# A two-block network on one core: gated linear attention over pairs of chunks, normalised tiles in full value from ACT, and a table that shifts the planner's order

## The chip, the core and the metric

The kernel runs on one core of a Trainium2 chip. The engines are named as in the profile: PE multiplies matrices (PEld loads its weights), DVE works on vectors, ACT evaluates functions and casts, POOL (GpSimd) does some of the element-wise work, and SP issues DMAs. The metric is the device time of one run in microseconds (us); lower is better.

## What is computed

512 tokens of width 1024 go through two networks in a row, with float32 inputs and outputs. The first has two layers: a short convolution with a SwiGLU feed-forward stage (`ffn0` below), then a forgetting attention of 16 heads ("fox" in the code) with a second one (`ffn1`). Each sub-block ends with a layer norm over the residual. The second network has a mixing block of four heads of latent attention (MLA) beside four heads of gated linear attention, a third feed-forward stage (`ffn2`) and a gated projection. The part that the change rewrites is the gated linear attention, which runs once forward and once backward over the tokens:

```python
def gla_chunkwise(q, k, v, logf):            # CHUNK = 64, 8 chunks
    b = jnp.cumsum(logf.reshape(B, H, N, CHUNK, DK), axis=3)
    b_last = b[:, :, :, -1:, :]
    b_mid = b[:, :, :, CHUNK // 2 - 1:CHUNK // 2, :]
    A = einsum('bhntd,bhnsd->bhnts', q * exp(b - b_mid), k * exp(b_mid - b)) * mask
    o_intra = einsum('bhnts,bhnsv->bhntv', A, v)
    kv = einsum('bhnsd,bhnsv->bhndv', k * exp(b_last - b), v)
    # scan over chunks: state = exp(b_last) * state + kv; s_before is the state ahead of a chunk
    o_inter = einsum('bhntd,bhndv->bhntv', q * exp(b), s_before)
    return (o_intra + o_inter).reshape(B, H, S, DV)
```

## The kernel before

Activations lie transposed, 128 features on the partitions and 512 tokens along the free axis. A float32 product of full size is made of three fp32r matmuls, (high, high), (low, high) and (high, low): every weight unit `raw` of 128x1024 is cast by ACT to `whi`, and `wlo` = `raw` - `whi` is made by DVE or POOL; an activation tile is split in the same way into `...h` and `...l`. The smaller products of the gated linear attention are plain float32 matmuls.

The program is not written in the order in which it runs. Class `Build` records some ten thousand operations in a `Recorder`; `plan()` is a list scheduler that goes through a model of the engines with a cost for each operation and picks, on each engine, the ready operation with the lowest `prio`; `issue()` emits them in that order. Hence nearly every instruction has one line in the profile, that of `issue()` (L575), and a load of ACT's function table has L578. The priority is

```python
        op.prio = op.i - op.shift - OFFSETS.get(op.group, 0)
```

where `op.i` is the place in the recorded program, and `OFFSETS` is empty, so the order is that of the recording as far as data, buffers and engines allow. The planner may give some of DVE's `tensor_tensor` operations to POOL (`to_pool`); it lets no POOL operation start while a DVE operation with two SBUF inputs runs, and the other way round. `issue()` puts a table load right behind the last ACT operation that uses the old table. PSUM has 8 banks in classes `g`, `s` and `o`; four weight units (`WB`) are held at once.

What the change touches, by names in the profile:

- `split_scaled` is the end of each layer norm. For a tile `x` (features 128, tokens 256) ACT writes `hm0h`, `hm1h`, ... (the normalised tile times gain plus offset, rounded to fp32r); DVE writes the same in full value as `hm00e`, `hm10e`, ..., and subtracts, giving `hm0l`, `hm1l`, .... `ln_tiles` calls it 16 times in the norms behind the convolution block, `ffn0` and the attention; the queries' input `hq` takes it 8 times at 512 tokens.
- `gla_prep` makes, for head h and direction d, the decayed tiles from the running sum `b`: `gl01qi`, `gl01bm` (queries and keys relative to the middle of a chunk), `gl01bl` (keys to the end of a chunk), `gl01qb` (queries from the start of a chunk).
- `gla_scores` multiplies queries and keys over 128 tokens at a time, four matmuls into `gs01A`; `copy_predicated` with the mask `gmask` keeps the two 64x64 blocks on the diagonal, in their triangle. `gs01kt` transposes `gl01bl`, and ACT copies it to `gs01kd`.
- `gla_states` multiplies keys and values of each 64-token chunk (`gl01kv`, seven matmuls over 64 partitions, in two PSUM banks), makes seven states `gl01st` (one ACT copy and six DVE `scalar_tensor_tensor`, each needing the one before), and adds to the output `gpo` four matmuls of the masked scores `gat` with the values and seven of 64 columns with the states.
- In the mixing block `gt` are the gate projections, `gvt` the transposed values, `MS` the scores of MLA with `kns`, `krs` (keys) and `qns`, `qrs` (queries), `mx` the row maxima of MLA's softmax, `rqn`, `rkn` and `gr` sums for norms, `mx0` to `mx6` also (with h and l) the split outputs of the heads, and `wo` the output projection `w_o2`, of which partial sums start before all heads are done. `ffn2` starts with `pg` and `pu`.
- In the attention of block 1, `pk`, `pq`, `pv` are projections, `S` the scores, `Pa`, `Pm`, `Pb` the softmax parts after DVE has multiplied them by the reciprocal sums, `tp` their transposes, `PT` the split transposes, `po` the products with the values, and `Ftp` the transpose of the running sum `F` of the forget gates.

Of the kernel before, what the change touches and what calls it, by code (L numbers as in the profile page):

```python
# [85 lines left out]
    ("SP", "ACT"): 130, ("SP", "DVE"): 130, ("SP", "PE"): 130, ("SP", "POOL"): 130, ("SP", "SP"): 130,  # L86
}
FREE_LAT = {"g": 220, "s": 220, "o": 220, "whi": 200, "wlo": 200}
OFFSETS = {}
LOOK = 4000  # L90
DMA_LOOK = 250
POOL_LAG = -1000.0
# [101 lines left out]
class Recorder:  # L194
# [96 lines left out]
    def cost(self, op, ins, outs):  # L291
        n = op.name
        size = 1
        for d in outs[0].shape[1:] if outs and isinstance(outs[0], View) else ():
            size *= d
        if n == "dma_start":
            v = next(x for x in outs + ins if isinstance(x, View))
            byts = 4
            for d in v.shape:
                byts *= d  # L300
            op.dma = byts / 359.0
            return {"SP": 60, "ACT": 60, "POOL": 1040}[op.eng]
        if op.eng == "PE":
            dt = ins[0].dtype
            if n == "transpose":
                return 109
            if dt == F32:
                return 4 + max(4 * size / 2.4, 156)
            return 13.4 + max(size / 2.4, 95) if dt == F32R else 3 + size / 2.4
        psum = any(x.tile.cls in PSUM_CLS for x in ins)  # L310
        cols = sum(1 for x in ins if isinstance(x, View) and x.idx.size == 1)
        if op.eng == "ACT":
            return (51 if psum else 94) + 0.8333 * size + 93 * (cols + ("accum_out" in op.kw))
        if op.eng == "POOL":
            return 200 + 2.13 * size if n == "tensor_tensor" else 36 + 0.8333 * size
        if n in ("tensor_tensor_reduce", "tensor_reduce"):
            size = int(ins[0].idx.size)
        if n == "tensor_tensor_reduce":
            return 180 + 1.0417 * size + 61 * cols
        if n in ("tensor_scalar", "tensor_copy", "memset") and not psum:  # L320
            return 68 + 0.5208 * size + 61 * cols
        if n == "reciprocal":
            return 68 + 6.4 * size
        return 68 + 1.0417 * size + (61 * cols if size > 1 else 0)
# [264 lines left out]
class Build:  # L589
# [291 lines left out]
    def split_scaled(self, d, g, b, hl, sl, name):  # L881

        nc = self.nc
        nc.scalar.activation(hl[0][:, sl], d[:, sl], AF.Identity, bias=b, scale=g)
        e = self.f(name + "e", (P, sl.stop - sl.start))
        nc.vector.tensor_scalar(e, d[:, sl], g, b, ALU.mult, ALU.add)
        nc.vector.tensor_tensor(hl[1][:, sl], e, hl[0].bitcast(F32)[:, sl], ALU.subtract)

    def scaled(self, d, g, b, sl=slice(0, T)):
# [841 lines left out]
    def mla_scores(self, h, proj):  # L1731
# [2 lines left out]
        scale = float(192 ** -0.5)  # L1734
        mx = self.small(f"mx{h}", 4)
        rs = self.small(f"mrs{h}", 4)
        Ps = []
        for i in range(4):
            tb = slice(i * P, (i + 1) * P)
# [77 lines left out]

    def gla_prep(self, h, gates):

        nc = self.nc  # L1820
        kl, q, _, _ = gates
        out = []
        for d in range(2):
            k, b = kl[d]
            nm = f"gl{h}{d}"
            step = 1 - 2 * d
            mid, last = (31, 63) if d == 0 else (32, 0)
            b3 = b.chunks(64)
# [12 lines left out]
            self.act(bl, bl, AF.Exp)  # L1841
            nc.vector.tensor_tensor(bl, bl, k, ALU.mult)
            self.act(b, b, AF.Exp)
            qb = self.f(nm + "qb")
            nc.vector.tensor_tensor(qb, b, q, ALU.mult)
            out.append((qi, bm, bl, b, qb))
        return out

    def gla_scores(self, h, prep):
# [1 line left out]
        nc = self.nc  # L1851
        res = []
        for d in range(2):
            qi, ki, kd_, _, _ = prep[d]
            nm = f"gs{h}{d}"
            pa = self.ps("s", nm + "A", (P, 4, P))
            for p in range(4):
                sl = slice(p * P, (p + 1) * P)
                nc.tensor.matmul(pa[:, p, :], ki[:, sl], qi[:, sl], start=True, stop=True)
            nc.vector.copy_predicated(self.at[d], self.gmask[:, d:d + 1, :].to_broadcast((P, 4, P)), pa)  # L1860
            kd = self.f(nm + "kd", (P, 4, P))
            nc.scalar.copy(kd, self.to_token_ps(kd_, nm + "kt"))
            res.append(kd)
# [5 lines left out]
    def gla_states(self, h, gates, prep, kds):  # L1869
# [1 line left out]
        nc = self.nc  # L1871
        v = gates[2]
        po = self.ps("o", f"gpo{h}")
        first = True
        for d in range(2):
            b, qb = prep[d][3:]
            nm = f"gl{h}{d}"
            kd = kds[d]
            last = 63 * (1 - d)
            order = list(range(8)) if d == 0 else list(range(7, -1, -1))  # L1880

            pk = [self.ps("s", nm + f"kv{i}", (P, 4, P)) for i in range(2)]
            for c in order[:7]:
                rw = slice(64 * (c % 2), 64 * (c % 2) + 64)
                nc.tensor.matmul(pk[c % 2][:, c // 2, :], kd[rw, c // 2, :], v[rw, c // 2, :],
                                 start=True, stop=True)
            for p in range(4 if d == 0 else 0):
                nc.tensor.matmul(po[:, p * P:(p + 1) * P], v[:, p, :], kds[2][:, p, :],
                                 start=first, stop=False)
                first = False  # L1890
            st = [self.f(nm + f"st{i}", (P, 4, P)) for i in range(2)]
            S = None
            for i, c in enumerate(order[:7]):
                new = st[i // 4][:, i % 4, :]
                kvc = pk[c % 2][:, c // 2, :]
                if S is None:
                    nc.scalar.copy(new, kvc)
                else:
                    col = c * 64 + last
                    nc.vector.scalar_tensor_tensor(new, S, b[:, col:col + 1], kvc, ALU.mult, ALU.add)  # L1900
                S = new
                n = order[i + 1]
                nc.tensor.matmul(po[:, n * 64:(n + 1) * 64], S, qb[:, n * 64:(n + 1) * 64],
                                 start=False, stop=(d == 1 and i == 6))
        return po

    def gla_out(self, h, gates, po):
# [144 lines left out]
```

## Time and profile before

| | |
|---|---|
| Median of the runs | 1939.76 us (1939.32 to 1940.83, 3 runs) |
| Profiled execution: device time | 1939.52 us |
| Profiled execution: span, first to last instruction | 1937.8 us |
| Outside the span | 1.7 us |
| PE busy | 1893.9 us (98%) |
| DVE busy | 1284.3 us (66%) |
| ACT busy | 817.4 us (42%) |
| POOL busy | 190.3 us (10%) |
| Mean granted clock of PE | 0.989 |

A busy PE is not a PE at its peak: records of consecutive matmuls overlap, and at half clock each lasts longer. So the starts of consecutive matmuls give what one costs. The stages follow each other in time: convolution block to about 203 us, `ffn0` to 550, attention of block 1 to 835, `ffn1` to 1215, mixing block to 1529, `ffn2` and the gated projection to the end.

### The profile page before, as it was taken

What the parts mean: (1) busy time and instruction counts of PE and PEld (TensorE: products, weight loads), DVE (VectorE), ACT (ScalarE), POOL (GpSimd) and SP (SyncE); (2) the same over time, 40 slices, a digit from 0 to 9 for tenths busy, and PEclk for the clock granted to TensorE, in tenths of its full rate; (3) what the DMA queues carried; (4) which work ended last, traced back from release to release, by engine and by line L of the source; (5) the groups of instructions that cost most, each with busy time, mean ns of one, the idle gap of its engine ahead of it and who ended that gap; (6) DMA issues with size and microseconds to landing.
All of it is one profiled execution on the core that took longest, in us unless ns stands there. A gap on an engine that the chain in (4) does not pass through costs nothing.

```text
span 1937.8 us, 24555 instructions
## 1 busy us (share of the span) xinstructions
PE 1893.9 (98%) x9382; PEld 1593.3 (82%) x9382; DVE 1284.3 (66%) x2208; ACT 817.4 (42%) x1344; POOL 190.3 (10%) x148
## 2 busy tenths in 40 slices
PE   9999999999999989999999999999999999999999
PEld 7888888888888778898888888877877888888887
DVE  8877976566579788894533335999898644334445
ACT  5322523122346667553322232686684533123333
POOL 0000100000010332210000000132151000000000
PEclk9999999999999899999999999999998999999999
DMA  9675277566434112323222222422111222222232
GB/s 350 224 249 173 99 241 251 187 233 228 142 108 153 58 64 88 120 66 131 99 94 96 97 98 79 140 82 82 44 55 44 98 98 98 98 98 94 94 139 76
DMA packets 76470, 245.55 MB, mean 127 GB/s; under 512 B 8496, under 2 KB 9776, under 8 KB 76352
## 3 DMA queue, kind: packets, MB, share of 16 engines
q1 hardware_dynamic: 76352, 243.98, 36.6%
q8 instruction: 73, 1.20, 0.3%
q14 instruction: 45, 0.37, 0.1%
HBM read 235.53 MB, written 8.42 MB: 126 GB/s over the span
## 4 chain that ended last, share of the span: by engine, by line
PE 57%; DVE 7%; ACT 2%; issue 1%; DVEq 0%; ACTq 0%
PE pu L575 12%; PE pg L575 12%; PE pd L575 9%; PE gt L575 4%; PE ffn_down L575 2%; PE wo L575 2%; PE pl L575 2%; PE attn_o L575 1%; DVE axr L575 1%; PE pv L575 1%; PE po L575 1%; PE pq L575 1%; PE MS L575 1%; PE tp L575 1%; PE pk L575 1%; PE S L575 1%
## 5 line engine op out<-in xcount | busy, mean ns | idle before, releaser
L575 ACT CAST whi<-raw 128x1024 fp32r<-128x1024 f32 (+1 forms) x313 | 326.1, 1043 | 598.5 <-PE pd L575 139.1
L575 DVE TENSOR_TENSOR wlo<-raw,whi 128x1024 fp32r<-128x1024 f32 (+1 forms) x286 | 349.8, 1224 | 321.0 <-ACT whi L575 316.9
L575 POOL TENSOR_TENSOR wlo<-raw,whi 128x1024 fp32r<-128x1024 f32 x27 | 65.4, 2423 | 1281.7 <-ACT whi L575 1251.5
L575 DVE CUSTOM_DVE_ANT_0 aj<-ada,cact,adab 128x1024 bf16<-128x1024 f32 x96 | 126.3, 1322 | 30.0 <-DMA ada<-in_wada 29.4
L575 DVE TENSOR_TENSOR s<-pu,s 128x512 f32<-128x512 f32 x44 | 30.1, 689 | 76.5 <-PE pu L575 76.5
L575 DVE TENSOR_TENSOR S<-S,sq 128x512 f32<-128x512 f32 (+1 forms) x62 | 36.7, 591 | 1.6 <-ACT sq L575 1.4
L575 ACT ACTIVATE s<-s 128x512 f32<-128x512 f32 x22 | 13.9, 632 | 54.1 <-DVE s L575 54.1
L575 ACT ACTIVATE s<-pg 128x512 f32<-128x512 f32 x44 | 26.0, 591 | 23.2 <-PE pg L575 23.0
L575 DVE CUSTOM_DVE_ANT_0 G<-S,G 128x128 f32<-128x128 f32 (+3 forms) x64 | 30.6, 484 | 1.6 <-PE S L575 0.9
L575 DVE TENSOR_TENSOR xr<-pd,xr 128x512 f32<-128x512 f32 x16 | 11.0, 690 | 26.9 <-PE pd L575 26.9
L575 DVE TENSOR_SCALAR G<-Fm,fneg 128x128 f32<-128x128 f32 x64 | 25.9, 410 | 0.9 <-PE po L575 0.5
L575 ACT ACTIVATE sq<-axr 128x256 f32<-128x256 f32 (+1 forms) x33 | 15.1, 466 | 23.1 <-DVE axr L575 23.1
L575 DVE TENSOR_SCALAR G<-Fb,fneg 128x128 f32<-128x128 f32 (+2 forms) x48 | 23.6, 491 | 1.3 <-ACT Pa L575 0.6
L575 DVE TENSOR_TENSOR s<-pg,rfr 128x512 f32<-128x512 f32 x22 | 15.2, 691 | 12.0 <-PE pg L575 12.0
L575 DVE TENSOR_TENSOR u<-pu,rfr 128x512 f32<-128x512 f32 x22 | 15.2, 691 | 11.8 <-PE pu L575 11.7
L575 POOL TENSOR_TENSOR Fm<-Fb,cmask 128x512 f32<-128x512 f32 x14 | 18.6, 1334 | 27.7 <-DVE PT_2l L575 9.1
L575 PE MATMUL tp<-ident,Pa 128*128 128x128 f32 x64 | 17.2, 294 | 3.2 <-DVE Pa L575 3.1
L575 PE MATMUL pg<-hm0l,whi 128*128 128x512 f32 (+1 forms) x48 | 18.0, 376 | 1.9 <-DVE hm0l L575 1.9
L575 PE MATMUL pg<-hm0h,whi 128*128 128x512 f32 (+1 forms) x48 | 18.0, 378 | 1.3 <-ACT hm0h L575 1.3
L575 ACT ACTIVATE Pa<-G,negm 128x128 f32<-128x128 f32 (+1 forms) x32 | 16.2, 505 | 6.8 <-DVE negm L575 4.7
L575 ACT ACTIVATE sq<-x 128x256 f32<-128x256 f32 (+1 forms) x19 | 9.8, 518 | 21.6 <-DVE x L575 21.5
L575 PE MATMUL pg<-hm0h,wlo 128*128 128x512 f32 (+1 forms) x48 | 18.0, 376 | 0.6 <-DVE wlo L575 0.6
(3680 smaller groups left out, 6298.7 us busy)
## 6 DMA issues: line engine op xcount, KB each, us to landing
raw<-in_wpack SPq DMA_DIRECT2D x309, 512.0 KB, 3.5
ada<-in_wada SPq DMA_DIRECT2D x96, 512.0 KB, 4.2
ada<-in_wada SPq DMA_DIRECT2D x32, 256.0 KB, 6.0
Fb<-fd SPq DMA_DIRECT2D x16, 256.0 KB, 4.5
x<-in_xT SPq DMA_DIRECT2D x8, 256.0 KB, 6.0
pd<-pple SPq DMA_DIRECT2D x8, 256.0 KB, 6.0
xd<-x SPq DMA_DIRECT2D x8, 256.0 KB, 2.6
axr<-xd SPq DMA_DIRECT2D x8, 256.0 KB, 5.1
```

The lines of the kernel that those rows point to most:

```text
L575: getattr(getattr(nc, op.unit), op.name)(*[get(x) for x in op.args], **{k: get(x) for k, x in op.kw.items()})
```

## The change

Four parts. First, `OFFSETS` gets some 150 entries, one per group of operations, from -1420 to 5570 places; a positive one lets the group go earlier. This moves instructions on every engine. Second, two of the planner's costs are raised: that of small float32 matmuls and that of the scan. Third, `split_scaled` writes the full value with a second ACT activation in place of DVE's `tensor_scalar`. Fourth, the gated linear attention takes chunks in pairs of 128 tokens: the prepared keys and queries reach to the ends of a pair (six products of 256 elements and one of 4 columns, `dec`, in place of two of 512), each direction adds four matmuls `gs01A<-gl01x` (64 columns by 64) for the block of scores between the two chunks of a pair, two memsets per head widen the mask, `gl01kv` are three matmuls over all 128 partitions in one bank, and there are three states and three matmuls of 128 columns with them. The four `gat` matmuls stand first.

```diff
-OFFSETS = {}
+OFFSETS = {
+    "attn_o_0": 830, "attn_o_1": -20, "attn_o_2": 300, "attn_o_3": 30, "attn_o_ln0": -20, "attn_o_ln1": -20,
...
+    "q2": -80, "q3": 50, "q5": -10, "q6": 3750, "q7": 950, "sc1": -20, "sc2": 20, "sc3": -80, "sc4": -50,
+    "sc5": 70, "sc6": 2420, "score0": 650, "score1": -130, "score2": 50, "score3": 300, "state0": 4020,
...
-                return 4 + max(4 * size / 2.4, 156)
+                return 4 + max(4 * size / 2.4, 193)
...
+        if n == "tensor_tensor_scan":
+            return 68 + 2.0833 * size
...
-        nc.vector.tensor_scalar(e, d[:, sl], g, b, ALU.mult, ALU.add)
+        nc.scalar.activation(e, d[:, sl], AF.Identity, bias=b, scale=g)
...
+        nc.gpsimd.memset(self.gmask[:64, 0, 64:], 1)
+        nc.gpsimd.memset(self.gmask[64:, 1, :64], 1)
...
-            nc.vector.tensor_tensor(bl, bl, k, ALU.mult)
             self.act(b, b, AF.Exp)
+            bp, lp = b.chunks(P), bl.chunks(P)
+            x = self.f(nm + "x", (P, 2, 256))
+            kx, qx = x[:, 0, :].chunks(64), x[:, 1, :].chunks(64)
+            nc.vector.tensor_tensor(kx, lp[:, :, near], k3[:, :, near], ALU.mult)
+            nc.vector.tensor_tensor(lp[:, :, far], lp[:, :, far], k3[:, :, far], ALU.mult)
+            nc.vector.tensor_tensor(lp[:, :, near], kx, bp[:, :, e1:e1 + 1].to_broadcast((P, 4, 64)), ALU.mult)
+            nc.vector.tensor_tensor(qx, bp[:, :, far], q3[:, :, far], ALU.mult)
             qb = self.f(nm + "qb")
-            nc.vector.tensor_tensor(qb, b, q, ALU.mult)
-            out.append((qi, bm, bl, b, qb))
+            qp = qb.chunks(P)
+            nc.vector.tensor_tensor(qp[:, :, near], bp[:, :, near], q3[:, :, near], ALU.mult)
+            nc.vector.tensor_tensor(qp[:, :, far], qx, bp[:, :, e0:e0 + 1].to_broadcast((P, 4, 64)), ALU.mult)
+            dec = self.small(nm + "dec", 4)
+            nc.vector.tensor_tensor(dec, bp[:, :, e0], bp[:, :, e1], ALU.mult)
+            out.append((qi, bm, bl, dec, qb, x))
...
+            for p in range(4):
+                sl = slice(p * 64, (p + 1) * 64)
+                nc.tensor.matmul(pa[near, p, far], x[:, 0, sl], x[:, 1, sl], start=True, stop=True)
...
-            pk = [self.ps("s", nm + f"kv{i}", (P, 4, P)) for i in range(2)]
-            for c in order[:7]:
-                rw = slice(64 * (c % 2), 64 * (c % 2) + 64)
-                nc.tensor.matmul(pk[c % 2][:, c // 2, :], kd[rw, c // 2, :], v[rw, c // 2, :],
-                                 start=True, stop=True)
...
+            pk = self.ps("s", nm + "kv", (P, 4, P))
+            for c in order[:3]:
+                nc.tensor.matmul(pk[:, c, :], kds[d][:, c, :], v[:, c, :], start=True, stop=True)
+            st = self.f(nm + "st", (P, 4, P))
...
-            for i, c in enumerate(order[:7]):
+            for i, c in enumerate(order[:3]):
...
-                    nc.vector.scalar_tensor_tensor(new, S, b[:, col:col + 1], kvc, ALU.mult, ALU.add)
+                    nc.vector.scalar_tensor_tensor(new, S, dec[:, c:c + 1], pk[:, c, :], ALU.mult, ALU.add)
...
-                nc.tensor.matmul(po[:, n * 64:(n + 1) * 64], S, qb[:, n * 64:(n + 1) * 64],
-                                 start=False, stop=(d == 1 and i == 6))
+                nc.tensor.matmul(po[:, n * P:(n + 1) * P], S, qb[:, n * P:(n + 1) * P],
+                                 start=False, stop=(d == 1 and i == 2))
```

What the table does to the order is seen at three places. The first is PE near the end of the mixing block, ahead of the scores `MS` of MLA's last head. Before, one matmul of the output projection stands there:

```order
L575 MATMUL gs30A_13103<-gl30qi_12803,gl30bm_12582 128x128 x4
L575 MATMUL gs30kt_13119<-ident_74,gl30bl_12588 128x128 x4
L575 MATMUL gs31A_13125<-gl31qi_13047,gl31bm_13044 128x128 x4
L575 MATMUL gs31kt_13133<-ident_74,gl31bl_13051 128x128 x4
L575 MATMUL wo2_13140<-mx0h_12823,whi227_12425 128x512
L575 MATMUL gl30kv0_13148<-gv3_12596,gs30kd_13127 128x128 x4
L575 MATMUL MS3_0_13157<-kns3h_13142,qns3h_13091 128x512
L575 MATMUL MS3_0_13157<-kns3l_13154,qns3h_13091 128x512
```

Now:

```order
L606 MATMUL wo2_13086<-mx4h_12713,wlo228_12591 128x512
L606 MATMUL wo0_13056<-mx2h_12879,whi228_12569 128x512
L606 MATMUL wo1_13066<-mx2h_12879,whi228_12569 128x512
L606 MATMUL wo2_13086<-mx2h_12879,whi228_12569 128x512
L606 MATMUL wo4_13160<-mx0h_12432,whi231_13121 128x512
L606 MATMUL wo4_13160<-mx0l_12824,whi231_13121 128x512
L606 MATMUL MS3_0_13168<-kns3h_13165,qns3h_13151 128x512
L606 MATMUL MS3_0_13168<-kns3l_13170,qns3h_13151 128x512
L606 MATMUL MS3_0_13168<-kns3h_13165,qns3l_13162 128x512
```

Ahead of `MS3_0` there now stands a run of matmuls of the output projection `wo`, of which only the last are shown (32 from the second `rkn3ps` on; before there is one), and the scores `gs30A` and `gs31A` of the linear attention are apart from it.

The second is ACT at the layer norm behind the convolution block; `out1r` and `out1a` belong to its second half of tokens. Before:

```order
L575 ACTIVATE hm0h<-x_123,m0B,m0G 128x256
L575 ACTIVATE hm1h<-x_195,m0B,m0G 128x256
L575 ACTIVATE conv_out1r_1889<-conv_outvar_1859 128x256
L575 ACTIVATE conv_out1r_1889<-conv_out1r_1889 128x256
L578 ACT_TABLE_LOAD
L575 ACTIVATE conv_out1a<-conv_out1r_1889 128x256
L575 ACTIVATE hm2h<-x_235,m0B,m0G 128x256
```

Now:

```order
L606 ACTIVATE hm0h<-x_123,m0B,m0G 128x256
L606 ACTIVATE hm00e<-x_123,m0B,m0G 128x256
L606 ACTIVATE conv_out1r_1884<-conv_outvar_1863 128x256
L606 ACTIVATE hm1h<-x_194,m0B,m0G 128x256
L606 ACTIVATE conv_out1r_1884<-conv_out1r_1884 128x256
L609 ACT_TABLE_LOAD
L606 ACTIVATE hm10e<-x_194,m0B,m0G 128x256
L606 ACTIVATE conv_out1a<-conv_out1r_1884 128x256
L606 ACTIVATE hm2h<-x_234,m0B,m0G 128x256
```

Each rounded tile (`hm0h`) is followed by its full value (`hm00e`), and the table load that stood behind both `hm0h` and `hm1h` now stands between `hm1h` and `hm10e`.

The third is PE in the attention of block 1, where the first transpose `tp` of the first pair of heads stands. Before:

```order
L575 MATMUL pv_0_5453<-whi_5320,hk5h 128x256
L575 MATMUL pv_0_5453<-wlo_5338,hk5h 128x256
L575 MATMUL tp_0_5567<-ident,Pa_5402 128x128
L575 MATMUL pv_0_5453<-whi_5320,hk5l 128x256
L575 MATMUL pv_1_5466<-whi_5320,hk5h 128x256
L575 MATMUL pv_1_5466<-wlo_5338,hk5h 128x256
```

Now:

```order
L606 MATMUL pk_5327<-hk4h,wlo_5149 128x512
L606 MATMUL S_1_5551<-k1a,q1a 128x256
L606 MATMUL S_1_5551<-k1l,q1az 128x256
L606 MATMUL pk_5327<-hk5h,whi_5132 128x512
L606 MATMUL pk_5327<-hk5l,whi_5132 128x512
L606 MATMUL tp_0_5562<-ident,Pa_5393 128x128
L606 MATMUL pk_5327<-hk5h,wlo_5149 128x512
L606 MATMUL tp_0_5562<-ident,Pm_5439 128x128
```

Before, the transpose stands among the value projections `pv`; now all of these are ahead of it, the scores `S` of the next heads are too, and the key projection `pk` stands beside it.

## Rows read from the trace of the kernel before

**Rows 1.** The page, part 1: busy time, share of the span and instructions of each engine.
```profile
PE 1893.9 (98%) x9382; PEld 1593.3 (82%) x9382; DVE 1284.3 (66%) x2208; ACT 817.4 (42%) x1344; POOL 190.3 (10%) x148
```

**Rows 2.** Windows of the span: window, length; busy us per engine, granted clock, DMA.
```profile
610.00:700.00 90.00, 81.42 (x412) 67.10 (x412) 71.65 (x190) 51.50 (x121) 31.53 (x21) 0.89 0.31 103
...
1405.00:1450.00 45.00, 41.67 (x300) 34.36 (x297) 40.71 (x84) 38.54 (x77) 25.44 (x19) 1.00 0.17 59
1450.00:1475.00 25.00, 20.77 (x83) 17.67 (x83) 22.86 (x36) 9.50 (x19) 9.07 (x7) 0.66 0.13 43
...
1530.00:1900.00 370.00, 370.00 (x1634) 306.39 (x1633) 168.61 (x194) 117.60 (x140) 4.79 (x2) 1.00 0.29 103
```

**Rows 3.** The same view, of four stretches in which TensorE's clock was halved.
```profile
647.90:658.10 10.20, 9.59 (x32) 7.00 (x31) 8.38 (x33) 3.72 (x12) 0.00 (x0) 0.50 0.01 5
688.80:695.70 6.90, 5.28 (x18) 4.11 (x19) 5.81 (x19) 1.80 (x4) 1.42 (x4) 0.51 0.00 0
1450.00:1460.20 10.20, 10.12 (x46) 9.89 (x46) 10.07 (x21) 6.10 (x12) 4.85 (x5) 0.50 0.01 2
1467.10:1473.90 6.80, 5.91 (x14) 4.65 (x15) 5.35 (x10) 1.56 (x4) 0.00 (x0) 0.50 0.45 154
```

**Rows 4.** Waits of PE: who waited for whom: us in total, times, longest us.
```profile
PE tp L575 <- DVE Pm L575: 3.5, 2, 2.9
PE tp L575 <- DVE Pa L575: 3.1, 4, 1.5
...
PE Ftp L575 <- DVE F L575: 2.5, 1, 2.5
PE MS L575 <- DVE kns3l L575: 2.4, 1, 2.4
...
PE gpo L575 <- DVE gl20st L575: 1.9, 1, 1.9
PE MS L575 <- DVE mx L575: 1.8, 1, 1.8
```

**Rows 5.** Timeline of 1455 to 1475 us: start, us, engine, operation, names, [idle before].
```profile
1456.36 0.68 DVE L575 TENSOR_TENSOR gl31bm<-gl31bm,gz 128x512 f32<-128x512 f32 x1
...
1459.35 1.73 POOL L575 TENSOR_TENSOR mx0l<-mo,mx0h 128x512 fp32r<-128x512 f32 x1
...
1460.30 0.60 PE L575 MATMUL gs31kt<-ident,gl31bl 128*128 128x128 f32 x4
...
1463.23 1.75 DVE L575 TENSOR_TENSOR kns3l<-kn,kns3h 128x512 fp32r<-128x512 f32 x1
...
1465.03 0.50 PE L575 MATMUL MS<-kns3l,qns3h 128*128 128x512 f32 x1 [2.37 <-DVE kns3l L575]
```

**Rows 6.** Timeline of PE, second head of the gated linear attention.
```profile
1425.85 1.16 PE L575 MATMUL gl11kv<-gv,gs11kd 64*128 64x128 f32 x14
...
1429.44 1.16 PE L575 MATMUL gpo<-gat,gv 128*128 128x128 f32 x8 [0.84 <-DVE gat L575]
...
1433.33 1.73 PE L575 MATMUL gpo<-gl11qb,gl11st 128*128 128x64 f32 x14
```

**Rows 7.** The states of one direction, by tile: duration in ns, minimum, median, maximum.
```profile
L575 DVE SCALAR_TENSOR_TENSOR gl20st<-gl20st,sg_0e,gl20kv x6: 330/333/333, 1449.3 to 1451.9; 128x128 f32<-128x128 f32 x6
```

**Rows 8.** Timeline of 202 to 210 us, the layer norm behind the convolution block.
```profile
203.11 0.60 ACT L575 ACTIVATE hm0h<-x,m0B,m0G 128x256 fp32r<-128x256 f32 x1
...
203.86 0.69 DVE L575 TENSOR_SCALAR hm00e<-x,m0G,m0B 128x256 f32<-128x256 f32 x1
...
205.07 1.28 ACT L578 ACT_TABLE_LOAD   x1
...
205.41 0.41 DVE L575 TENSOR_TENSOR hm1l<-hm10e,hm1h 128x256 fp32r<-128x256 f32 x1
...
206.72 0.28 PE L575 MATMUL pg<-hm1l,whi 128*128 128x256 f32 x1
```

**Rows 9.** Timeline of PE in the attention of block 1: the first transpose.
```profile
638.62 0.30 PE L575 MATMUL tp<-ident,Pa 128*128 128x128 f32 x1 [0.76 <-DVE Pa L575]
```

More of the change, by code (lines that the diff above doesn't have):

```diff
@@ L88 @@
 FREE_LAT = {"g": 220, "s": 220, "o": 220, "whi": 200, "wlo": 200}
-OFFSETS = {}
+OFFSETS = {
[27 rows of a table added]
+}
 LOOK = 4000
@@ L1821, in gla_prep @@
         kl, q, _, _ = gates
+        q3 = q.chunks(P)
         out = []
@@ L1827, in gla_prep @@
             mid, last = (31, 63) if d == 0 else (32, 0)
-            b3 = b.chunks(64)
+            near, far = slice(64 * d, 64 * d + 64), slice(64 - 64 * d, P - 64 * d)
+            e0, e1 = (63, 127) if d == 0 else (64, 0)
+            b3, k3 = b.chunks(64), k.chunks(P)
             nc.vector.tensor_tensor_scan(b[:, ::step], self.cmk, b[:, ::step], 0.0, ALU.mult, ALU.add)
@@ L1853, in gla_scores @@
         for d in range(2):
-            qi, ki, kd_, _, _ = prep[d]
+            qi, ki, kd_, _, _, x = prep[d]
             nm = f"gs{h}{d}"
+            near, far = slice(64 * d, 64 * d + 64), slice(64 - 64 * d, P - 64 * d)
             pa = self.ps("s", nm + "A", (P, 4, P))
@@ L1873, in gla_states @@
         po = self.ps("o", f"gpo{h}")
-        first = True
+        for p in range(4):
+            nc.tensor.matmul(po[:, p * P:(p + 1) * P], v[:, p, :], kds[2][:, p, :],
+                             start=(p == 0), stop=False)
         for d in range(2):
-            b, qb = prep[d][3:]
+            dec, qb = prep[d][3:5]
             nm = f"gl{h}{d}"
-            kd = kds[d]
-            last = 63 * (1 - d)
-            order = list(range(8)) if d == 0 else list(range(7, -1, -1))
-            pk = [self.ps("s", nm + f"kv{i}", (P, 4, P)) for i in range(2)]
-            for c in order[:7]:
-                rw = slice(64 * (c % 2), 64 * (c % 2) + 64)
-                nc.tensor.matmul(pk[c % 2][:, c // 2, :], kd[rw, c // 2, :], v[rw, c // 2, :],
-                                 start=True, stop=True)
[L1887 to L1891, printed above, removed]
+            order = list(range(4)) if d == 0 else list(range(3, -1, -1))
+            pk = self.ps("s", nm + "kv", (P, 4, P))
+            for c in order[:3]:
+                nc.tensor.matmul(pk[:, c, :], kds[d][:, c, :], v[:, c, :], start=True, stop=True)
+            st = self.f(nm + "st", (P, 4, P))
@@ L1892, in gla_states @@
             S = None
-            for i, c in enumerate(order[:7]):
-                new = st[i // 4][:, i % 4, :]
-                kvc = pk[c % 2][:, c // 2, :]
+            for i, c in enumerate(order[:3]):
+                new = st[:, i, :]
                 if S is None:
-                    nc.scalar.copy(new, kvc)
+                    nc.scalar.copy(new, pk[:, c, :])
                 else:
-                    col = c * 64 + last
-                    nc.vector.scalar_tensor_tensor(new, S, b[:, col:col + 1], kvc, ALU.mult, ALU.add)
+                    nc.vector.scalar_tensor_tensor(new, S, dec[:, c:c + 1], pk[:, c, :], ALU.mult, ALU.add)
```

24 rows, old and new, of the table OFFSETS are left out of this document.

## The prediction, made before the changed kernel ran

> **What bounds the kernel now.** I read the busy shares first: PE is busy for 98% of the span, DVE for 66% [rows 1], so PE sets the time and only two things can shorten it: fewer matmuls, or less time lost by PE. Next the windows, to see where PE loses. In the feed-forward stages it loses nothing: from 1530 to 1900 us it is busy for all 370 us at full clock [rows 2], so no order can gain there. The losses sit where DVE is nearly full too: from 610 to 700 us PE is idle for 8.6 of 90 us at a mean clock of 0.89, and from 1450 to 1475 us for 4.2 of 25 us at 0.66, while DVE works 22.9 of these 25 us [rows 2]. The granted clock says why such a place costs more than its idle time: in four stretches of 6.8 to 10.2 us it is 0.5, that is 1.2 in place of 2.4 GHz [rows 3]; work in them takes twice as long, so half of PE's busy time there is lost. The waits of PE then name the links [rows 4]: transposes `tp` of the attention waiting for DVE's `Pm` and `Pa`, `Ftp` for `F`, and in the mixing block `MS` for `kns3l` and `mx`, `gpo` for `gl20st`. In the timeline [rows 5] the reader sees one such link: `kns3l` takes DVE 1.75 us, where an operation of the same shape takes 0.68 us at 1456.36; POOL worked on `mx0l` and its like meanwhile, 1.73 us each.
>
> **What is there to be had.** Mixing block, end: waits 2.4 + 1.9 + 1.8 = 6.1 us [rows 4], and half of the busy time at half clock, (10.12 + 5.91) / 2 = 8.0 us [rows 3]: 14.1 us. Attention: waits of `tp` 3.5 + 3.1 = 6.6 us [rows 4], and (9.59 + 5.28) / 2 = 7.4 us of clock [rows 3]: 14.0 us; the wait of `Ftp`, 2.5 us, stands apart. What follows is a sum against the profiled execution's own 1939.52 us, which is 0.24 us below the median of the runs, so both can be compared with the forecast.
>
> **Matmuls of the linear attention.** Per head and direction: seven products over half the partitions took 1.16 us and four full ones 1.16 us, 0.29 each [rows 6]; three full ones make 0.87, a gain of 0.29. Seven products with states took 1.73 us, 0.25 each [rows 6]; three of 128 columns make 0.87, a gain of 0.86. The four cross products of 64 columns are not in the trace: like the state products (also 64 columns) they cost 4 x 0.25 = 1.0 us; four transposes at 0.60 [rows 5] and four full products at 1.16 us are the ends. I take 1.0, since column count and type agree. Per direction -0.15 us (-0.55 to +0.01), for eight **-1.2 us** (-4.4 to +0.1). So the pairs hardly save PE anything.
>
> **DVE and POOL in the linear attention.** Per direction two products of 512 elements, 0.68 us each [rows 5], become six of 256 at 0.41 [rows 8] and a product of 4 columns, not in the trace, between 0 and a state's 0.33 [rows 7]: +1.1 to +1.4. Four state steps of 0.33 [rows 7] go: -1.3. DVE's load is the same; what shrinks is the chain that `gpo` waits for, from six steps to two. The planner moves more to POOL: along the order, POOL has 82 products in the mixing block where it had 60, 22 more at up to 1.73 us [rows 5], 38 us, in windows where DVE is at 90% (40.7 of 45 us) and POOL at 25.4 us [rows 2].
>
> On that the trace speaks against the change: with POOL at work DVE's `kns3l` went from 0.68 to 1.75 us [rows 5]. The Trainium skill, GPSIMD Engine Reference, section 1 (Specifications), says that GpSimd shares its SBUF interfaces with VectorE and contends with DVE instructions of two SBUF inputs; the trace agrees at this place, 1.75 against 0.68 us. By that rule the mixing block would gain nothing, and the sum would be 10.5 us worse; this is the second rival below.
>
> **The end of the mixing block.** Two moves meet the 14.1 us. Between `rkn3ps` and `MS3` the new order puts 32 matmuls of `wo` where there was one; at the 370 us / 1634 = 0.226 us that a matmul of this kind takes in `ffn2` [rows 2], that is 7.2 us of work that needs nothing from DVE, against waits of 2.4 and 1.8 us [rows 4]. And the shorter state chain takes 4 x 0.33 = 1.3 of the 1.9 us of `gl20st`. The work itself is not less: what stands as cover now is missing at the end, where `wo` ran without a gap. I do not expect all to go, since DVE remains full there and what is late next is a softmax row maximum or `gat`; I take three quarters, **-10.5 us** (-14.1 to +4; the loss is one more wait of 1.9 us with clock of 2 us).
>
> **The attention of block 1.** The order moves the first `tp` of seven of the eight pairs of heads forward: counted in matmul time behind `Ftp`, from 26.0 to 21.8 us in the first pair, 150.1 to 132.3 in the seventh, by 2 to 7 us in five others, while the sixth moves back by 9. DVE's place of the reciprocals ahead of `Pa` moves by -2 to +4 us along its own order. In the trace the first `tp` starts at 638.62 after a wait of 0.76 us for `Pa` [rows 9], so DVE ends last there, and an earlier place for `tp` means a longer wait. Against that, `pk` and `pq` now stand ready beside the transposes, where before the value projections were used up, and what PE does not do ahead of `tp` it does behind it. I take a little over a quarter of the 14.0 us, **-4 us** (-14 to +20). `Ftp` keeps its 2.5 us, as `F` hangs on the same chain.
>
> **The layer norms.** The full value moves from DVE (0.69 us, `hm00e`) to ACT (0.60 us, `hm0h`) [rows 8]; per norm 16 of each. DVE is relieved, and PE's first wait, for `hm0l`, falls. But ACT's order is now `hm0h`, `hm00e`, `out1r`, `hm1h`, `out1r`, table load, `hm10e`: from 203.11, 0.6 us for each activation of which two are 0.4 gives a load from about 205.7 to 207.0 where it was at 205.07 [rows 8], `hm10e` to 207.6 and `hm1l`, 0.41 later, at 208.0. PE took `hm1l` at 206.72 [rows 8]: +1.2 us. After the attention the same load stands in the norm; half of that, +0.6. The norm after `ffn0` has no load: 0. Sum **+1.8 us** (0 to +4, if the new idle of some 2 us ahead of `hm1l` were followed by half clock as others were).
>
> **Feed-forward stages.** They lose nothing now [rows 2]; the new order interleaves output tiles and holds more weight units at once, of four. **+0.5 us** (0 to +4): cover is PE's own queue, and a late weight unit would show at once.
>
> Sum: -1.2 - 10.5 - 4 + 1.8 + 0.5 = -13.4, and 1939.5 - 13.4 = **1926.1 us**. With neighbouring values of the two large terms it runs from 1918 to 1934.
>
> **Rivals.** *Both stalls go.* The table need only clear the two places named: -14.1 - 14.0 - 1.2 + 2.3 = -27.0, 1912.5 us. For it: 32 matmuls of cover against waits of 2.4 us. Against it: DVE is at 90% and more in both places.
>
> *DVE with POOL bounds the mixing block.* 22 more POOL products each stretch a DVE product by up to 1.75 - 0.68 = 1.1 us, 24 us of DVE, more than the 15 us (22 x 0.68) that it hands over. Then `MS`, `gat` and `mx` come as late as now and the cover only moves the wait: 0 in place of -10.5, 1936.6 us.
>
> *The attention gets slower.* One mechanism: `tp` is issued ahead of `Pa`. Two half-clock stretches of 6.9 and 10.2 us lie among the eight pairs now [rows 3]. If there are six, four more stretches of 10.2 us lose 5.1 us each: +20.4, and with the rest of the sum 1939.5 + 20.4 - 10.5 - 1.2 + 2.3 = 1950.5 us. It decides where `Pa` comes some 2 us behind PE: the longest waits that stand at such stretches are 1.9, 2.4 and 2.9 us [rows 4]. For it: the first pair waits already [rows 9] and its `tp` moves 4 us forward, DVE's reciprocals only 2.
>
> *The pairs don't do what they say*, if the cross products cost 1.16 us: PE saves nothing, 1927.3 us, inside the forecast's range.
>
> **How the numbers follow.** Forecast 0.48 (nearly all of it faster), both stalls gone 0.22 (faster), DVE and POOL 0.16 (1936.6 lies at the edge: 0.04 faster, 0.11 same, 0.01 slower), slower attention 0.13; 0.01 for the rest. A measurement of this kernel can tell 0.2%, 3.9 us, from no change. Faster: 0.46 + 0.22 + 0.04 = 0.72; same: 0.01 + 0.02 + 0.11 = 0.14; slower: 0.14. The range leaves out the slower attention above (0.13) and the lower third of the case that both stalls go below (0.07), 0.20 together: 1909 to 1944.
>
> **What would show it.** In the changed kernel's trace: no wait of `MS` for `kns3l` and full clock between the last `gpo` of head 2 and `MS3` (the -10.5); clock and waits of `tp` between 610 and 835 us (the -4); a wait of about 2 us of `pg` for `hm1l` behind the convolution (+1.2); 370 of 370 us in `ffn2`. The sum is wrong if the mean clock is lower than 0.989, if DVE's products beside POOL's grow in number in the mixing block, or if PE shows gaps in `ffn1` or `ffn2`.

## The result and the profile after

The changed kernel took 1920.93 us (median of 4 runs, 1918.61 to 1923.07) against 1940.3 us for the kernel before, run beside it: a ratio of 0.9899 with a 95% interval of 0.9882 to 0.9916. The forecast was 1926.1 us with a range of 1909 to 1944. The profiled execution of the changed kernel is the shortest of its runs (1918.61 us, span 1916.9), so differences between the two profiles add up to 1.5 us more than those of the medians.

The first thing to read is where in the span the time went. PE's first matmul of each stage gives that. In the timeline of PE after the change (start, us, engine, operation, names, and in brackets what PE waited for):

```profile
203.03 0.39 PE L606 MATMUL pg<-hm0h,whi 128*128 128x256 f32 x1 [1.74 <-ACT hm0h L606]
...
572.99 0.33 PE L606 MATMUL pf<-hk0h,narrow 128*64 128x256 f32 x1 [1.31 <-ACT hk0h L606]
...
610.59 0.29 PE L606 MATMUL Ftp<-ident,F 16*128 16x16 f32 x2
...
833.15 0.47 PE L606 MATMUL pg<-hm0h,whi 128*128 128x256 f32 x1
...
1203.20 0.39 PE L606 MATMUL cq<-hx0h,whi 128*128 128x256 f32 x1 [1.61 <-ACT hx0h L606]
...
1507.44 0.39 PE L606 MATMUL pg<-hf0h,whi 128*128 128x512 f32 x1
```

The same starts before were 203.76, 572.58, 610.03, 845.72, 1215.49 and 1529.04 us; these starts, and not the rounder bounds given for the kernel before, part the stages from here on. The lengths between them, here and below called by these names (the rest ends with PE's last matmul):

| us | to ffn0 | ffn0 | to `Ftp` | attention | ffn1 | mixing block | rest |
|---|---|---|---|---|---|---|---|
| before | 203.8 | 368.8 | 37.4 | 235.7 | 369.8 | 313.5 | 404.0 |
| after | 203.0 | 370.0 | 37.6 | 222.6 | 370.1 | 304.2 | 404.4 |
| change | -0.7 | +1.1 | +0.2 | -13.1 | +0.3 | -9.3 | +0.4 |

Two stages made the gain, the attention more than the mixing block; I had expected -4 and -11.7. The windows of the span after (busy us of PE, PEld, DVE, ACT, POOL, then the granted clock and DMA) answer to [rows 2] and [rows 3]:

```profile
610.00:700.00 90.00, 84.76 (x491) 71.70 (x489) 80.04 (x224) 65.55 (x153) 33.03 (x22) 0.98 0.29 96
1400.00:1440.00 40.00, 36.46 (x248) 30.43 (x248) 38.30 (x66) 27.30 (x54) 20.38 (x19) 1.00 0.23 80
1440.00:1460.00 20.00, 14.82 (x62) 10.16 (x60) 19.87 (x34) 7.58 (x14) 4.73 (x4) 0.83 0.12 41
1530.00:1900.00 370.00, 370.00 (x1632) 305.24 (x1631) 162.64 (x188) 111.95 (x134) 10.26 (x5) 1.00 0.28 99
```

From 610 to 700 us the clock rose from 0.89 to 0.98, and PE has 491 instructions in the window where it had 412. That is where the attention gained: from 700 us to the end of the stage the clock is full in both kernels. But ahead of the last head's `MS` (1440 to 1460 us) PE still stands idle for 5.2 of 20 us at a clock of 0.83, with DVE full. Of half clock, two stretches in each of the two stages in [rows 3], one in each is left; in the same view:

```profile
680.20:684.20 4.00, 4.00 (x17) 3.33 (x17) 2.89 (x7) 2.20 (x6) 0.00 (x0) 0.57 0.00 0
1448.00:1455.80 7.80, 4.38 (x12) 2.92 (x12) 7.80 (x13) 3.55 (x7) 4.17 (x3) 0.56 0.00 0
```

The waits of PE (who waited for whom: us, times, longest) answer to [rows 4]:

```profile
PE tp L606 <- DVE Pm L606: 2.7, 2, 1.9
...
PE MS L606 <- DVE gl30st L606: 1.6, 1, 1.6
PE pg L606 <- DVE hm1l L606: 1.6, 1, 1.6
PE gpo L606 <- DVE gl01st L606: 1.5, 1, 1.5
PE mtp L606 <- DVE MP L606: 1.5, 2, 0.9
PE gs31A L606 <- DVE gl31x L606: 1.3, 1, 1.3
...
PE gpo L606 <- DVE gl21st L606: 0.9, 1, 0.9
...
PE MS L606 <- DVE kns3l L606: 0.9, 1, 0.9
```

`tp` no longer waits for `Pa`, `Ftp` no longer for `F`. The wait of `pg` for `hm1l` is new, as forecast. `MS` waits again, now for `gl30st`.

### The profile page after: what moved, and what is told of

The parts are those of the page before. It is cut to its first block, busy times and chain, and to the rows that moved or that the text cites. A ratio compares the mean times of both kernels' runs of the same rounds, so it can differ in the third digit from the quotient of the medians.

```text
span 1916.9 us, 24374 instructions
## 1 busy us (share of the span) xinstructions
PE 1876.1 (98%) x9318; PEld 1573.6 (82%) x9318; DVE 1255.9 (66%) x2146; ACT 842.3 (44%) x1400; POOL 205.8 (11%) x170
## 5 line engine op out<-in xcount | busy, mean ns | idle before, releaser
L606 POOL TENSOR_TENSOR wlo<-raw,whi 128x1024 fp32r<-128x1024 f32 x29 | 71.4, 2465 | 1016.0 <-ACT whi L606 872.9
L606 DVE TENSOR_TENSOR S<-S,sq 128x512 f32<-128x512 f32 (+1 forms) x61 | 36.5, 598 | 1.0 <-ACT sq L606 0.7
L606 DVE TENSOR_SCALAR G<-Fm,fneg 128x128 f32<-128x128 f32 x64 | 20.8, 332 | 0.8 <-PE tp L606 0.4
L606 PE MATMUL pg<-hm1l,whi 128*128 128x512 f32 (+1 forms) x48 | 18.0, 375 | 1.6 <-DVE hm1l L606 1.6
L606 POOL TENSOR_TENSOR Fm<-Fb,cmask 128x512 f32<-128x512 f32 x13 | 17.6, 1362 | 13.2 <-PE S L606 4.7
L606 PE MATMUL pg<-hm3l,whi 128*128 128x512 f32 (+1 forms) x48 | 17.9, 374 | 0.5 <-DVE hm3l L606 0.5
L606 DVE TENSOR_SCALAR G<-Fb,fneg 128x128 f32<-128x128 f32 (+2 forms) x48 | 18.1, 377 | 0.2
```

The costliest lines, as they stand in the source:

```text
L606: getattr(getattr(nc, op.unit), op.name)(*[get(x) for x in op.args], **{k: get(x) for k, x in op.kw.items()})
```

## The experiments

Two theories stood at the start. A: the order (the table) makes the gain, in the attention above all. B: the operations make it, the pairs of chunks and the full value on ACT. The stage lengths are read from the starts of the same matmuls as above, one profile each. Kernels with the same order in the mixing block differ there by up to 4 us from profile to profile (304.2 and 307.8 below), so less than that is not read as a difference in that stage. PE's waits in this stage are nearly the same in these two, the changed kernel and e4; what differs is the clock, which in e4 is halved once more near 1410 us and stays halved here until 1461.6 us, not 1455.8:

```profile
1448.00:1461.60 13.60, 10.28 (x34) 7.72 (x34) 12.60 (x22) 3.10 (x6) 4.17 (x3) 0.50 0.33 104
```

| us (medians in the last column) | ffn0 | to `Ftp` | attention | ffn1 | mixing block | median |
|---|---|---|---|---|---|---|
| e1 table without the new operations | 371.4 | 36.5 | 232.0 | 372.4 | 327.8 | 1951.4 |
| e2 new operations, no table | 369.5 | 36.8 | 237.2 | 368.9 | 309.7 | 1935.5 |
| e3 before + attention's entries | 369.1 | 36.0 | 233.8 | 369.2 | 317.7 | 1938.4 |
| e4 after, table loads later | 368.5 | 37.7 | 222.6 | 368.6 | 307.8 | 1919.4 |
| e5 after, full value on DVE, order kept | 372.7 | 40.5 | 220.9 | 375.4 | 306.3 | 1930.7 |
| e6 new operations + attention's entries | 369.5 | 37.6 | 220.9 | 368.9 | 301.6 | 1911.6 |
| e7 new operations + mixing block's entries | 369.4 | 36.8 | 236.7 | 370.2 | 312.5 | 1938.0 |
| e8 after, POOL's products on DVE | 369.8 | 37.6 | 222.5 | 370.1 | 308.8 | 1924.2 |
| e9 as e6, 64-token chunks | 370.8 | 37.6 | 220.9 | 368.9 | 313.9 | 1923.9 |
| e10 new operations + both stages' entries | 369.4 | 37.6 | 222.5 | 370.2 | 312.9 | 1925.4 |
| e11 after without the mixing block's entries | 369.8 | 37.6 | 222.5 | 369.3 | 307.2 | 1920.6 |
| e12 after without softmax normalisation | 369.8 | 37.6 | 222.5 | 370.1 | 301.9 | 1915.7 |

**e1, e2: table and operations apart.** e1 is the kernel before with the table and the two costs; e2 is the changed kernel with

```diff
-OFFSETS = { ... }
+OFFSETS = {}
```

> The kernel before with the table and the two planner costs, but with the linear attention in 64-token chunks and the full value on DVE. Theory A (the order makes the gain): the attention of block 1, from Ftp to the first matmul of ffn1, falls from 235.7 us to 223 to 227; the mixing block, to which the table was not fitted in this form, by 2 to 6 us; together 1922 to 1928 us. Theory B (pairs of chunks and the full value on ACT make it): both stages stay within 3 us of before, 1936 to 1942 us.

> The changed kernel with an empty table: pairs of chunks, full value on ACT, the two planner costs. Theory A: the attention of block 1 gains 0 to 3 us (DVE is relieved of eight operations for the queries' input), the mixing block 1 to 4 us, the layer norms lose 1 to 2; 1934 to 1940 us. Theory B: 1919 to 1925 us, with the attention near 223 us.

Measured: e1 1951.36 us, ratio to before 1.0053 (1.0035 to 1.007); e2 1935.47 us, 0.997 (0.996 to 0.998). Neither theory holds. The table alone makes the kernel slower: 3.7 us gained in the attention, 14.3 lost in the mixing block. The operations alone give 3.8 us in the mixing block, less than is read as a difference there, and nothing in the attention, as theory A had it for e2. The two parts gain 19 us together, and apart the one loses 11 and the other wins 5, so they are not additive.

**e3, e6: the attention's entries alone.** e3 puts the 33 entries of the attention's groups (`fox`, `logf`, `kv`, `v`, `q`, `sc`, `val`, `attn_o`) into the kernel before, e6 into the changed kernel in place of the whole table.

```diff
-OFFSETS = { ... 150 entries }
+OFFSETS = { ... 33 entries }
```

> The kernel before with the 33 entries of the table that belong to the attention of block 1, nothing else. Theory A: that stage alone falls from 235.7 to 223 to 228 us, all others stay within 1 us; 1927 to 1933 us. If the gain of that stage needs the relief of DVE by ACT, it stays at 232 us or more, above 1935 us in all.

> The changed kernel with only the 33 table entries of the attention of block 1. If its gain is local to the stage (these entries plus the full value on ACT): 222 to 226 us there, the mixing block 307 to 312 us as without a table, total 1921 to 1927 us. If the entries hang on the order of the stages ahead: 230 us or more there, total above 1929 us.

Measured: e3 1938.42 us, ratio 0.999 (0.9981 to 0.9999), the attention at 233.8 us; e6 1911.58 us, 0.985 (0.9835 to 0.9865), the attention at 220.9. So the entries work only in an order that was planned with the full value on ACT (e1 has the entries and the two new costs, without ACT, and 232.0 us), and there they need no other entry and no pairs of chunks: in every other kernel that has both (after, e4, e8, e9, e10, e11, e12) the stage is 220.9 to 222.6 us; those at 222.5 and 222.6 have the half-clock stretch near 680 us, those at 220.9 don't. All these kernels have the two new costs as well, which were not tried apart. With ACT but without them it is 236.7 and 237.2 (e7, e2). e2's waits of PE say what the entries remove:

```profile
PE tp L578 <- DVE Pa L578: 9.0, 7, 2.3
PE MS L578 <- ACT kns3h L578: 6.2, 1, 6.2
```

Seven times a transpose waits for `Pa`, 9.0 us in all; with the entries that wait is gone from the list. e6 is also the best kernel of this study, 9 us ahead of the changed one: with the 117 other entries the kernel is that much slower.

**e5: is it ACT's help or the order?** The order of the changed kernel is kept; only the 56 full values are issued on DVE, at the same places.

```diff
+        if op.name == "activation" and op.args[0].tile.name in FULL:
+            nc.vector.tensor_scalar(get(op.args[0]), get(op.args[1]), get(op.kw["scale"]), get(op.kw["bias"]),
+                                    ALU.mult, ALU.add)
```

> The changed kernel with its order kept, but the 56 full values issued on DVE as before, at the same places. If ACT's help to DVE makes the attention's gain: that stage, 222.6 us in the changed kernel, goes to 228 to 234 us and the total to 1926 to 1932 us. If the fitted order makes it and DVE had room: 222 to 225 us, total 1918 to 1923 us; ffn0 then gets shorter by 0 to 1.2 us, since ACT reaches hm1h and the table load earlier.

Measured: 1930.68 us, ratio 0.9949 (0.9934 to 0.9964), in the band that I had given to ACT's help, but by another way: the attention stays at 220.9 us. The loss is 2.7 us in ffn0, where the clock is halved from 204.9 to 211.4 us, 2.9 ahead of `Ftp` and 5.3 in ffn1, where one weight tile comes late from DVE:

```profile
PE pg L616 <- DVE wlo L616: 3.4, 1, 3.4
...
PE pq L616 <- DVE hq6l L616: 1.9, 1, 1.9
PE pg L616 <- DVE hm0l L616: 1.8, 2, 0.9
```

None of the full values is computed in the attention but ffn1's first at its very end: in the changed kernel the last of the queries', `hq7e`, starts at 606.37 us, 4 us ahead of `Ftp`. So e5 tests whether that relief, ahead of the stage, is needed in it, and it is not; the entries just belong to the order that the planner finds with ACT's cost in its model. In the norms ACT's help is real as soon as the order counts on it.

**e4: the table load in the norms.** The load moves from behind the last operation of the old table to ahead of the first of the new one, in ffn0 and ffn1.

```diff
-            load_at[prev] = s
+            load_at[i - 1 if order[i].group.startswith(("ffn_gate0", "ffn_gate1")) else prev] = s
```

> The changed kernel with the two table loads that stand in the layer norms of ffn0 and ffn1 put right ahead of the first operation that needs the new table; the order is the same. If the load between the rounded and the full tile makes PE wait for hm1l, that wait of 1.6 us falls below 0.5 and ffn0 gets 1.0 to 1.5 us shorter (370.0 to about 368.7), ffn1 up to 0.6; 1917 to 1920 us. If ACT's two operations per tile are what PE waits for, load or not, nothing moves by more than 0.3 us.

Measured: 1919.4 us, ratio 0.9884 (0.9864 to 0.9904); ffn0 368.5 us in place of 370.0 and ffn1 368.6 in place of 370.1. ACT's timeline shows `hm10e` right behind `out1r` where the load of 1.28 us stood (first two lines: the changed kernel; then e4):

```profile
204.61 1.28 ACT L609 ACT_TABLE_LOAD   x1
205.91 0.60 ACT L606 ACTIVATE hm10e<-x,m0B,m0G 128x256 f32<-128x256 f32 x1
...
204.15 0.59 ACT L606 ACTIVATE hm1h<-x,m0B,m0G 128x256 fp32r<-128x256 f32 x1
204.65 0.41 ACT L606 ACTIVATE conv_out1r<-conv_out1r 128x256 f32<-128x256 f32 x1
204.95 0.59 ACT L606 ACTIVATE hm10e<-x,m0B,m0G 128x256 f32<-128x256 f32 x1
```

The wait of `pg` for `hm1l` falls from 1.6 to 0.3 us. In ffn1 the load stood later, between `hm20e` and `hm3h` (836.90 us), and the waits of `pg` for `hm3h` and `hm3l`, 0.2 and 0.5 us, are gone. The load was the cause, and its cost is about 1.5 us in each of the two stages; 3 us of a total that scatters by 4 are not seen in the medians, the stages show it.

**e7, e10, e11: the mixing block's entries.** e7 has only the 30 entries of that stage, e10 these and the attention's, e11 all but these.

```diff
-OFFSETS = { ... 150 entries }
+OFFSETS = { ... 30, 63 or 120 entries }
```

> The changed kernel with only the 30 table entries of the mixing block. If these entries are local: the mixing block 302 to 308 us, the attention 236 to 239 us as without a table, total 1927 to 1933 us. If they hang on the order ahead: the mixing block above 310 us, total above 1934 us.

> The changed kernel with the entries of the attention and of the mixing block, and without the 87 of the other stages. If those 87 cost the 9 us between the changed kernel and the one with the attention's entries alone: 1910 to 1914 us, mixing block 300 to 304 us. If the mixing block's own entries cost it: 1916 to 1921 us, that stage 304 us or more.

> The changed kernel without the 30 entries of the mixing block. If the 87 entries of the other stages cost the 9 us: ffn0 and ffn1 370 us each as in the changed kernel, total 1916 to 1922 us. If the mixing block's own entries cost it: mixing block 300 to 303 us, total 1911 to 1915 us.

Measured: e7 1937.99 us, ratio 0.9982 (0.9973 to 0.9991); e10 1925.38, 0.9921 (0.9905 to 0.9938); e11 1920.61, 0.9896 (0.9881 to 0.9911). Among the kernels with pairs, with its own entries the mixing block takes 304.2 (after), 312.5 and 312.9 us, without them 309.7 (e2), 301.6 (e6) and 307.2 (e11). e6 and e2 have the same entries for this stage, none, and differ by 8 us; only entries of an earlier stage set them apart. So the planner's order of the mixing block follows how the model's time falls there, and the table's entries for it show no gain of their own: 3 us between e11 and the changed kernel, and 11 us lost between e6 and e10. The traces show one place where it is lost. At the last head's scores PE waits for `kns3h`, 6.2 us in e2, 6.1 in e7 and e10, 3.9 in e11; in e6 and in the changed kernel it does not. Of e10:

```profile
PE MS L578 <- ACT kns3h L578: 6.1, 1, 6.1
```

My e10 and e11 expectations both looked for one guilty group; there is none, e10 is slower than both e6 and the whole table.

**e9: the pairs of chunks by themselves.** e6 with the linear attention of before.

```diff
-        pk = self.ps("s", nm + "kv", (P, 4, P))
-        for c in order[:3]:
+        pk = [self.ps("s", nm + f"kv{i}", (P, 4, P)) for i in range(2)]
+        for c in order[:7]:
```

> The kernel with the attention's 33 table entries and the full value on ACT (1911.6 us in the run before), but with the linear attention in 64-token chunks as before the change. Attention 220 to 224 us by either theory. If the pairs of chunks are what shortens the mixing block: 310 to 318 us there in place of 301.6, total 1920 to 1928 us. If that stage only follows how the planner's order happens to fall: 298 to 308 us, total 1908 to 1918 us.

Measured: 1923.94 us, ratio 0.9911 (0.9896 to 0.9926); 12.4 us slower than e6, all of it in the mixing block (313.9 against 301.6). In the four kernels with 64-token chunks that stage takes 313.5 to 327.8 us, in the kernels with pairs 301.6 to 312.9, whatever the table. So the stage is shorter with them, by 12 us where nothing else in the program differs (e6 against e9). But the planner orders each kernel anew, and a new order alone moved this stage by 11 us (e6 against e10); how much of the 12 us is the pairs' own is not shown. Where e9 loses most is one wait of PE, at the last head's scores again:

```profile
PE MS L577 <- ACT krs3h L577: 8.9, 1, 8.9
```

**e8: POOL's products on DVE.** Order kept; 57 products of the mixing block move from POOL to DVE.

```diff
+        if op.unit == "gpsimd" and op.name == "tensor_tensor" and op.group.startswith(MIX_STAGE) \
+                and not op.args[0].tile.name.startswith("wlo"):
+            op.unit = "vector"
```

> The changed kernel with its order kept, but the products that POOL does in the mixing block (not those for weights) issued on DVE at the same places. If a product on POOL holds DVE up by about as much as it would cost there (1.1 us of stretch against 0.68 us), the mixing block changes by less than 4 us either way. If POOL is real help: some 75 products of 0.4 to 0.68 us, about 40 us of DVE work where DVE is busy for 90%, make the mixing block 15 to 40 us longer, total 1935 to 1960 us.

Measured: 1924.19 us, ratio 0.9916 (0.9899 to 0.9932), 3.3 us more than the changed kernel; the mixing block 308.8 us, 4.6 more in the profile and so hardly a difference. The windows over the stage, of the changed kernel and then of e8 (PE, PEld, DVE, ACT, POOL):

```profile
1203.20:1507.44 304.24, 291.63 (x1521) 239.69 (x1521) 282.48 (x484) 208.63 (x373) 89.13 (x68) 0.99 0.22 75
```

```profile
1203.24:1512.09 308.85, 294.20 (x1521) 239.44 (x1521) 295.56 (x541) 209.69 (x373) 17.50 (x11) 0.99 0.23 74
```

POOL does 72 us less and DVE only 13.1 us more, though it has 57 more instructions. At 0.41 to 0.68 us each, as they take on DVE in [rows 8] and [rows 5], these would be 23 to 39 us. So 10 us or more of what POOL takes off DVE it gives back by stretching DVE's own products: of those of 128x512 elements, 15 took over 0.8 us in the changed kernel and 5 in e8.

**e12: less work for DVE.** Order kept, the normalisation of MLA's softmax left out.

```diff
+        if op.unit in ("vector", "gpsimd") and op.name == "tensor_scalar" and op.args[0].tile.name.startswith("MP"):
+            continue
```

> The changed kernel with its order kept, without the 16 products with which DVE normalises MLA's softmax (12.2 us of DVE in the mixing block, 12 of the 16 ahead of the last head's scores); this leaves a part of the computation out. If DVE's total load is what PE ends up waiting for at the end of the mixing block: that stage falls from 304 to 308 us to 295 to 300 us, the total to 1910 to 1914 us. If the end waits for a chain of latencies there, with DVE only busy beside it: 302 us or more, total 1917 us or more.

Measured: 1915.71 us, ratio 0.9866 (0.985 to 0.9883); the total lies between my two bands. The median is 5.2 us below the changed kernel's; the mixing block takes 301.9 us, 2.3 less than in the profile of the changed kernel, its shortest run, and at the border that I had set for a chain of latencies. The waits ahead of `MS` stay:

```profile
PE MS L608 <- DVE gl30st L608: 1.9, 1, 1.9
PE gs31A L608 <- DVE gl31x L608: 1.4, 1, 1.4
...
PE MS L608 <- DVE kns3l L608: 0.9, 1, 0.9
```

12.2 us less of DVE's work took away the waits that hung on the normalised tiles themselves (`mtp` for `MP`, 1.5 us), brought PE to the last head's scores 3.5 us earlier (the matmul that waits for `kns3l` starts at 1443.80 us in place of 1447.25) and left those at the last head as they were: 1.9, 1.4 and 0.9 where they had been 1.6, 1.3 and 0.9. So DVE's load costs something, 2 to 5 us of these 12.2, but the stall there is a local chain on DVE, not its total load. The changed kernel's timeline shows the chain:

```profile
1446.51 0.69 DVE L606 TENSOR_TENSOR kns3l<-kn,kns3h 128x512 fp32r<-128x512 f32 x1
...
1449.26 0.68 DVE L606 TENSOR_TENSOR gl31bl<-sg_1e 128x512 f32<-128x512 f32 x1
...
1451.43 0.35 DVE L606 SCALAR_TENSOR_TENSOR gl30st<-gl30st,gl30dec,gl30kv 128x128 f32<-128x128 f32 x1
...
1451.84 0.80 PE L606 MATMUL MS<-kns3h,qns3h 128*128 128x512 f32 x1 [1.65 <-DVE gl30st L606]
...
1453.11 2.28 DVE L606 TENSOR_TENSOR wlo<-raw,whi 128x1024 fp32r<-128x1024 f32 x1
```

The second score tile of the last head starts 0.06 us after the last `gl30st`, the operation that reads `gl30kv` for the last time: both tiles are of PSUM class `s`, so it waited for that bank, and DVE did `gl31bl`, among others, ahead of `gl30st`. That the bank is the reason is read from this trace and the code; no run changed it alone.

## Why the prediction was right, step by step

The direction and the range were right; the forecast was 5.2 us too slow, 13.4 us of gain where 19.4 were measured. The terms were not all right, and three of them missed by 3 us or more, in both directions; that the total came as near as it did is in part luck.

- **Matmuls of the linear attention, -1.2.** Mis-sized. In the changed kernel three `kv` products took 0.84, three state products 0.83 and the four cross products, which the trace of before did not show, 0.68 us:

```profile
1406.56 0.68 PE L606 MATMUL gs11A<-gl11x 128*64 128x64 f32 x8
...
1428.47 0.84 PE L606 MATMUL gl21kv<-gv,gs21kd 128*128 128x128 f32 x6
...
1431.58 0.83 PE L606 MATMUL gpo<-gl20qb,gl20st 128*128 128x128 f32 x6
```

  Against 1.16 + 1.73 us in [rows 6] that is -0.54 per head and direction, -4.3 for eight, at the end of the range given. By the starts of the instructions, which are what a run of matmuls costs, it is more: 1.08 us (1405.62 to 1406.70) and 1.56 (1433.33 to 1434.89) before, against 0.60 (1406.56 to 1407.16), 0.60 (1428.47 to 1429.07) and 0.67 (1431.58 to 1432.25) now, -0.77 per head and direction and -6.2 for eight, outside the range. The step that failed is the choice of 1.0 us for the cross products; the lower bound, the transposes of [rows 5], was nearer.
- **The end of the mixing block, -10.5.** Together with the matmuls the stage gave -9.3 against -11.7, so the sum held, but by luck: without the matmuls -3 to -5 us are left for this term, less than half of it. I had said that `MS` would no longer wait for `kns3l` and the clock stay full. It waits, 0.9 us, and for `gl30st` 1.6, and from 1448 to 1455.8 us the clock is at 0.56. Of the 14.1 us there, waits of 1.6 + 1.3 + 0.9 and half of 4.38 us remain, 6.0 us; the 32 matmuls of cover did not fill the stall, which now stands behind the first score tile. Nor is DVE's total load the reason (e12), as I had argued, and the shorter state chain did not spare `gpo` its waits: 1.9 us for `gl20st` before, 1.5 for `gl01st` and 0.9 for `gl21st` now.
- **The attention, -4.** Mis-sized by 9 us; the mechanism, waits of `tp` and the clock behind them, was right. Of 14.0 us there remain 2.7 us of waits for `Pm` and half of 4.00 us, so 9.3 went. Another 1.6 us went that [rows 3] does not show: before, the clock was halved behind the wait for `F` too,

```profile
610.40:613.70 3.30, 3.30 (x9) 2.62 (x9) 3.20 (x6) 1.91 (x4) 0.00 (x0) 0.50 0.27 92
```

  and I had priced that place at the 2.5 us of its wait alone and expected it to stay. Some 2 of the 13.1 us stay without a row. That DVE is at 90% and more in both places was a wrong reading: here it is busy for 71.65 of 90 us, 80% [rows 2], and for 89% in the changed kernel, which is faster. I had set the earlier place of `tp` against DVE's unmoved reciprocals and expected a longer wait; instead the first `tp` came at 635.38 us with no wait for `Pa`, 3.2 us earlier than in [rows 9]. I had counted DVE's place along its own order only, as if it never waited; the first pair's last scores start earlier too, 16.2 us behind `Ftp` (626.79 us) in place of 17.6 (627.59). And DVE loses less between them and `Pa`. Before (first two lines), an operation of theirs took 2.05 us while POOL made a weight tile; in the changed kernel (third line) it takes 0.41 us, and POOL is idle from 628.35 to 637.71 us:

```profile
633.69 2.40 POOL L575 TENSOR_TENSOR wlo<-raw,whi 128x1024 fp32r<-128x1024 f32 x1 [0.18 <-ACT whi L575]
634.26 2.05 DVE L575 TENSOR_SCALAR G<-Fb,fneg 128x384 f32<-128x384 f32 x1 [0.63 <-ACT Pa L575]
...
631.88 0.41 DVE L606 TENSOR_SCALAR G<-Fb,fneg 128x384 f32<-128x384 f32 x1
```

  That is 1.6 of the 3.2 us. No run changed either of the two alone.
- **The layer norms, +1.8.** Right where the load stands behind the convolution: +1.2 forecast, +1.1 measured, and e4 shows the load to be the cause. ffn1 +0.3 in place of +0.6.
- **Feed-forward, +0.5.** `ffn2` has 370 of 370 us busy as before; the rest of the span +0.4.
- **The rivals.** DVE and POOL do hinder each other (e8: 72 us of POOL's work for 13.1 us of DVE's). The Trainium skill, GPSIMD Engine Reference, section 1 (Specifications), names the shared SBUF interfaces as the reason; e8 agrees with it, the conclusion that nothing would be gained was mine. The mixing block gained all the same, since what it waits for at its end is a few places and not the sum (e12). The 22 more products on POOL are not in the traces either: between the first matmuls of the mixing block and of `ffn2` POOL has 64 products, weight tiles included, where it had 53. The slower attention did not come: one half-clock stretch is left there, not six. The pairs do save PE time, 4 to 6 us by the matmuls above; the rest of the 12 us between e6 and e9 is waits and clock at the last heads, which I had not priced.

What stays open: why the planner's order of the mixing block differs by 8 us between e2 and e6. The traces show one place, e2's wait of 6.2 us for `kns3h`, not which decision turns it.

## What to carry to other kernels

A table that is fitted to a scheduler's output belongs to that program and that schedule: the same 33 entries shortened their stage by 16 us where the full value was planned on ACT (e6 against e2) and by 2 us where it was not (e3 against before). Before keeping such a table, try its parts; here 33 of 150 entries were 9 us better than all. And where PE waits at one place, removing work from the engine it waits for leaves that wait standing unless the work is in the chain that ends there: 12.2 us less on DVE left the three waits within 0.3 us of what they were (e12).

## What the runs showed of the hardware

In the mixing block 57 products on POOL relieved DVE by only 13.1 us (e8), about 0.23 us each, although one of 512 elements takes DVE 0.68 us when it is alone. An ACT table load of 1.28 us among the tiles of a norm cost PE about 1.5 us; ahead of the first function that needs it, it cost nothing that shows (e4). And half clock did not always last as long: 3.3 us at one place of the kernel before, where [rows 3] has 6.8 to 10.2, and, behind the same waits in the same order, about 7 us in the changed kernel and 13 in e4.
